# Norm gain on x, each token's norm at the exit of the projections, and x delivered transposed, in a hybrid retention and GLA layer

## The chip, the cores and the metric

The kernel runs on one core of a Trainium2 chip. The metric is the device time of one execution in microseconds (us), the median of three runs; a profile was taken of one further execution. Engines are named as in the profile: PE is the matmul engine (PEld its weight loads), DVE the vector engine, ACT the scalar engine, POOL the GpSimd engine, SP the engine that issues most DMAs.

## The reference

One layer over 512 tokens and 16 learned meta tokens ahead of them (528 rows of 1024 numbers), in float32:

```
u = x * rsqrt(mean(x*x) + eps) * norm_gain            # per token
rq, rk, rv, rg, gq, gk, gv, gg, glr, m_ret, m_gla = split(u @ w_in)
o_ret = groupnorm(retention(rope(rq), rope(rk), rv)) * silu(rg)          # 4 heads, 256 wide, values 512
log_a = log_sigmoid(glr @ w_gate_up + b_gate) / 16
o_gla = rmsnorm(gla(gq, gk, gv, log_a)) * silu(gg)                       # 4 heads, 128 wide, values 256
merged = sigmoid(m_ret) * (o_ret @ w_branch_ret) + sigmoid(m_gla) * (o_gla @ w_branch_gla)
out = rms_norm(x + merged @ w_out, final_norm_gain)[after the meta tokens]
```

The norm of a token is one number per row of u. It therefore commutes with every projection: (x * gain) @ w, scaled per row afterwards, is the same as u @ w.

## The kernel before

**Precision.** Every float32 product is done as three passes. `split` (L139 to L141) writes a rounded copy "hi" with ACT and the remainder "lo" with DVE; `mm3` (L151) or the loops in `quad` and `proj_a` then issue hi·hi, hi·lo and lo·hi. Tiles with `_h` and `_l` are such parts. `fh` and `fl` hold seven forms of the transposed activation (features on the 128 partitions, tokens along the row): three of its four blocks (`A11`, `A12`, `A22`; the fourth is `a21h`, `a21l`) and four sums of blocks (`S1` to `S4`).

**Projections.** `quad` (L198) does a 512-column projection with seven block products in place of eight, and needs the sums of blocks. `proj_a` (L276) and `proj_b` (L317) do plain projections and need the four blocks only. Products are pinned to a fixed order on PE; generators are woven by `weave`, so that small attention steps stand between large products. A scheduler fixes the order of the instructions of each engine when the program is built; on the chip each engine works through its list in that order.

**Start.** SP loads the five blocks of x and meta tokens, the gain (broadcast to all partitions, `ngb`) and the first weights `gv_w`. Per block (L432 to L455): ACT squares and sums a row (`sq`, `ss`), DVE and POOL turn the sum into 1/sqrt (`n_v`, `n_r`, L163 and L164), DVE multiplies the row by it and by the gain (`xn`, L439), PE transposes eight 128x128 pieces into PSUM (`xt`, L444), ACT and DVE split them into the forms and ACT keeps a plain copy `u` (L453). Then DVE makes the sums of blocks in tiles of their own (`s`, L472 to L475) and these are split. Beside this runs `gv0`, the first projection (`proj_b`, 96 matmuls of 512 columns), whose lo parts POOL makes (`gv_l`). It is followed by the gate's low-rank input `glr`, by `gq` and `gk` (`proj_a`, 96 matmuls each), with `forget_gates` (L483) woven in: `z` on PE, then Abs, Exp and Ln on ACT and the rest on DVE give `la`, the log of the forget gates.

**GLA and retention.** `gla_attention` (L604) needs `la`: matmuls `ge`, `gf` sum it, ACT takes exponentials (`gX`), DVE and POOL multiply by k and q (`gK`, `gQ`), PE makes scores `gc`. It is woven with `gg0`, a `quad` on columns of `gg`. Retention works per head: q, k with `rope`, the gate `rg`, scores (`ret_scores`, times a decay table), values `rv`, then `ret_attention`. `gates` (L931) makes `mr` and `mg` with four quads and multiplies the results onto the kept branch outputs (`kr`, `kg`, through DRAM). The output projection `wo` ends the kernel.

Of the kernel before, what the change touches and what calls it, by code (L numbers as in the profile page):

```python
# [18 lines left out]
F32 = mybir.dt.float32  # L20
# [86 lines left out]
def hybrid_kernel(ctx: ExitStack, tc: tile.TileContext, I, out: bass.AP):  # L107
# [18 lines left out]
    fh = [cp.tile([P, 4, HW], F32R, tag=f"fh{i}", name=f"fh{i}") for i in range(7)]  # L126
    fl = [cp.tile([P, 4, HW], F32R, tag=f"fl{i}", name=f"fl{i}") for i in range(7)]
# [3 lines left out]
    ggain = cp.tile([P, 16], F32, name="ggain")  # L131
# [7 lines left out]
    def split(hi, lo, src, eng=nc.vector):  # L139
        nc.scalar.copy(hi, src)  # L140
        eng.tensor_sub(lo, src, hi.bitcast(F32))  # L141
# [56 lines left out]
    def quad(cols, rows, name, evac, meta=None):  # L198
# [52 lines left out]
        nc.vector.tensor_sub(blk[0, 0], blk[0, 1], blk[0, 0])  # L251
# [23 lines left out]

    def proj_a(col, meta, name, evac):  # L276
# [33 lines left out]
    loaded = {}  # L310

# [5 lines left out]
    def proj_b(src, col, left, name, evac, meta=None):  # L317

        pss = [ppt(f"{name}_p{t}") for t in range(NTB)]
        psm = pat(f"{name}_pm") if meta is not None else None  # L320
        raws = []
        for q in range(4):
# [4 lines left out]
            if name == "gv0":  # L327
                for kk in range(2):
                    split(hi[:, kk, :], lo[:, kk, :], raw[:, kk, :], nc.gpsimd)
            else:  # L330
                split(hi, lo, raw)
            raws.append(raw)
# [9 lines left out]
            if psm is not None and q % 2 == 1:  # L342
                for g in range(4):
                    k = 2 * (q - 1) + g
                    nc.tensor.matmul(psm[32 * g:32 * g + 32], um[:, k, :], raws[q - 1 + g // 2][:, g % 2, :],
                                     start=q == 1, stop=q == 3)
            if q == 3 and psm is not None:
                late.append(lambda: meta(psm))
# [54 lines left out]
    gmask = g1.tile([P, 3, P], I32, name="gmask")  # L403

    xctx = ExitStack()
    xp = xctx.enter_context(tc.tile_pool(name="xp", bufs=2))


    blocks = [(I["x"][t * P:(t + 1) * P, :], P, t * P) for t in range(NTB)]
    blocks.append((I["meta_tokens"], NM, T))  # L410
    xts = []
    ngb = xp.tile([P, D], F32, name="ngb", bufs=1)
    for n, (src, rows, t0) in enumerate(blocks):
        xts.append(xp.tile([P, D], F32, tag="xt", name=f"xt{n}", bufs=5))
        nc.sync.dma_start(xts[n][:rows], src)
        if n == 0:
            nc.sync.dma_start(ngb, I["norm_gain"].to_broadcast([P, D]))
        if n < NTB:
            load_b(w_in, C_GV, n, "gv0")

    wzero = xp.tile([P, 512], mybir.dt.bfloat16, name="warm", bufs=1)
    nc.vector.memset(wzero, 0.0)
    wps = pat("warm_p")

    def warm(n):
        for _ in range(n):
            nc.tensor.matmul(wps, wzero[:, :P], wzero, start=True, stop=True)

    warm(14)
    nc.gpsimd.memset(um, 0.0)  # L430
    u = xp.tile([P, 2, 2, 4, HT], F32, name="u", bufs=1)
    for n, (src, rows, t0) in enumerate(blocks):  # L432
        xt = xts[n]
        sq = xp.tile([P, D], F32, tag="sq", name=f"sq{n}")
        ss = sp.tile([P, 1], F32, tag="ss", name=f"ss{n}")
        nc.scalar.activation(sq[:rows], xt[:rows], AF.Square, accum_out=ss[:rows])
        r = rstd_of(ss[:rows], D, rows, f"n{n}")
        xn = xp.tile([P, D], F32, tag="xn", name=f"xn{n}")
        nc.vector.scalar_tensor_tensor(xn[:rows], xt[:rows], r[:rows], ngb[:rows], op0=ALU.mult, op1=ALU.mult)  # L439
        for g in range(2):  # L440
            pt = pat(f"xt{n}_{g}")
            for e in range(4):
                k = 4 * g + e
                nc.tensor.transpose(pt[:, e * P:e * P + rows], xn[:rows, k * P:(k + 1) * P], ident[:rows, :rows])  # L444
            v = pt.rearrange("p (e t) -> p e t", e=4)[:, :, :rows]
            if rows == NM:
                nc.vector.tensor_copy(um[:, 4 * g:4 * g + 4, :NM], v)
                parts = [(th, 256, HT, v[:, :, HM * th:HM * (th + 1)]) for th in range(2)]
            else:
                parts = [(n // 2, (n % 2) * P, (n % 2 + 1) * P, v)]  # L450
            for th, c0, c1, w in parts:
                split(ah[th, g][:, :, c0:c1], al[th, g][:, :, c0:c1], w)
                nc.scalar.copy(u[:, th, g, :, c0:c1], w)  # L453
# [18 lines left out]
    nc.vector.tensor_sub(ss3, u[:, 0, 0], u[:, 1, 0])  # L472
# [604 lines left out]
```

## Time and profile before

| what | value |
|---|---|
| median of three runs | 822.9 us (822.75 to 823.49) |
| the profiled execution | 823.74 us, of which the span of the trace is 822.0 us |
| PE | busy 790.3 us (96%), 5466 matmuls |
| DVE | busy 541.5 us (66%) |
| ACT | busy 407.7 us (50%) |
| POOL | busy 147.3 us (18%) |
| granted PE clock, mean | 0.988 |
| DMA | 95.62 MB, 116 GB/s over the span |

The profile is one execution. Its page gives busy times, the span in 40 slices with the busy share of each engine in tenths, DMA queues, a chain of work followed back from the end, and the costliest groups of instructions. Further views used below: a table of stretches (busy time per engine in each), groups of instructions by line, and the instructions in order of time; there a row is start, duration, engine, line, operation, output<-input, and in brackets how long the engine was idle before and what ended it. In the chain's view a row is start, length and what, and since matmuls overlap in a pipeline, its lengths give the rate better than a single matmul's duration.

### The profile page before, as it was taken

Reading aid. Unit: us, or ns where it says so; the run is one execution under the profiler, and the core shown is the slowest. Engines: PE = TensorE matmul, PEld = TensorE weight load, DVE = VectorE, ACT = ScalarE, POOL = GpSimd, SP = SyncE. Lnnn points to the kernel's source line nnn. Section 1 sums busy time; section 2 is a strip of 40 time slices with the busy share of each in tenths; the row PEclk is TensorE's granted clock in tenths of the full one; section 3 lists DMA queues with packets and bytes.
Section 4 is the critical chain, followed back from the end, with each engine's and each line's share of the span. In section 5 each row is a group of like instructions: output and inputs, shape, how many; then the busy total and the mean of one; then the engine's idle time right before and its main releaser. Section 6 shows DMA issues by size and latency. Waiting matters only on the chain.

```text
span 822.0 us, 13635 instructions
## 1 busy us (share of the span) xinstructions
PE 790.3 (96%) x5466; PEld 719.3 (88%) x5466; DVE 541.5 (66%) x775; ACT 407.7 (50%) x673; POOL 147.3 (18%) x186
## 2 busy tenths in 40 slices
PE   6898999999999999999999999999999998999896
PEld 3687988998887999998999989999899998998685
DVE  3758666577643398766677576766757778885922
ACT  6564585357744336525445354453444555553422
POOL 4500243005331240013000141002410010021031
PEclk9998999999999999999999999999999999999999
DMA  9240330033335803521426237261472267589402
GB/s 282 82 115 26 90 90 3 26 103 103 111 120 143 193 26 103 176 82 65 143 76 185 72 72 151 66 198 57 85 146 71 84 218 230 179 184 249 146 0 103
DMA packets 84679, 95.62 MB, mean 116 GB/s; under 512 B 7988, under 2 KB 71732, under 8 KB 84616
## 3 DMA queue, kind: packets, MB, share of 16 engines
q1 hardware_dynamic: 78984, 86.36, 34.4%
q0 software_dynamic: 5632, 8.39, 7.0%
q8 instruction: 43, 0.70, 0.4%
q14 instruction: 20, 0.16, 0.1%
HBM read 77.96 MB, written 16.78 MB: 115 GB/s over the span
## 4 chain that ended last, share of the span: by engine, by line
PE 75%; DVE 6%; DMA 4%; ACT 4%; issue 2%; POOL 2%; SPq 0%; POOLq 0%; DVEq 0%; ACTq 0%
PE rk_p L297 6%; PE rg_b L225 6%; PE rq_p L297 6%; PE rv_b L225 5%; PE gk_p L297 3%; PE rg_c L225 3%; PE br_p L155 3%; PE br_p L152 3%; PE br_p L156 3%; PE rv_c L225 2%; PE mg_b L225 2%; DMA mk<-kept 2%; PE gg_b L225 2%; PE wo_p L152 2%; PE wo_p L156 2%
## 5 line engine op out<-in xcount | busy, mean ns | idle before, releaser
L164 POOL TENSOR_TENSOR g_r<-g_v,mhalf 128x1 f32<-128x1 f32 x16 | 10.3, 646 | 265.4 <-DVE g_v L163 265.4
L152 PE MATMUL br_p<-oh,br_h 128*128 128x512 f32 x128 | 50.1, 391 | 0.5 <-DVE mt L974 0.5
L155 PE MATMUL br_p<-ol,br_h 128*128 128x512 f32 x128 | 50.3, 393 | 0.0
L156 PE MATMUL br_p<-oh,br_l 128*128 128x512 f32 x128 | 50.1, 391 | 0.0
L141 DVE TENSOR_TENSOR rg_l<-rg_w,rg_h 128x1024 fp32r<-128x1024 f32 x24 | 30.0, 1252 | 17.9 <-ACT rg_h L140 17.9
L141 DVE TENSOR_TENSOR rv_l<-rv_w,rv_h 128x1024 fp32r<-128x1024 f32 x24 | 29.4, 1224 | 15.8 <-ACT rv_h L140 15.8
L914 ACT ACTIVATE on<-av,nm,g_r 128x512 f32<-128x512 f32 x16 | 12.5, 778 | 52.6 <-DVE nm L912 52.6
L140 ACT CAST rv_h<-rv_w 128x1024 fp32r<-128x1024 f32 x24 | 25.3, 1052 | 23.9 <-issue 7.3
L225 PE MATMUL rv_b<-rv_h,fh 128*128 128x256 f32 x128 | 36.3, 284 | 0.0
L225 PE MATMUL rg_b<-rg_l,fh 128*128 128x256 f32 x128 | 36.0, 281 | 0.0
L225 PE MATMUL rv_b<-rv_h,fl 128*128 128x256 f32 x128 | 36.0, 281 | 0.0
L225 PE MATMUL rv_b<-rv_l,fh 128*128 128x256 f32 x128 | 36.0, 281 | 0.0
L140 ACT CAST rg_h<-rg_w 128x1024 fp32r<-128x1024 f32 x24 | 25.2, 1052 | 21.6 <-PE br_p L155 11.6
L225 PE MATMUL rg_b<-rg_h,fl 128*128 128x256 f32 x128 | 35.9, 281 | 0.0
L225 PE MATMUL rg_b<-rg_h,fh 128*128 128x256 f32 x128 | 35.8, 280 | 0.0
L639 POOL COPY gto<-gX 128x1 f32<-128x1 f32 x16 | 8.5, 530 | 122.9 <-ACT gX L629 122.9
L152 PEld LDWEIGHTS br_p<-oh,br_h 128*128 128x128 f32 x128 | 24.0, 188 | 6.1 <-issue 0.9
L638 POOL TENSOR_TENSOR gQ<-gX,gq 128x512 f32<-128x512 f32 x16 | 28.3, 1768 | 3.9 <-ACT gX L631 3.9
L152 PE MATMUL wo_p<-wo_h,mh 128*128 128x512 f32 (+1 forms) x72 | 26.9, 374 | 2.0 <-DVE mt L974 2.0
L156 PEld LDWEIGHTS br_p<-oh,br_l 128*128 128x128 f32 x128 | 24.0, 188 | 5.2
L155 PEld LDWEIGHTS br_p<-ol,br_h 128*128 128x128 f32 x128 | 24.0, 188 | 5.0
L297 PE MATMUL rk_p<-fh,rk_h 128*128 128x264 f32 x96 | 27.6, 287 | 0.0
(490 smaller groups left out, 3098.2 us busy)
## 6 DMA issues: line engine op xcount, KB each, us to landing
rg_w<-in_w_in_dram SPq DMA_DIRECT2D x16, 512.0 KB, 4.2
rv_w<-in_w_in_dram SPq DMA_DIRECT2D x16, 512.0 KB, 3.9
br_w<-in_w_branch_ret_dram SPq DMA_DIRECT2D x16, 512.0 KB, 4.1
gv_w<-in_w_in_dram SPq DMA_DIRECT2D x8, 512.0 KB, 3.6
gg_w<-in_w_in_dram SPq DMA_DIRECT2D x8, 512.0 KB, 4.5
bg_w<-in_w_branch_gla_dram SPq DMA_DIRECT2D x8, 512.0 KB, 3.5
rq_w<-in_w_in_dram SPq DMA_DIRECT2D x8, 512.0 KB, 4.2
rk_w<-in_w_in_dram SPq DMA_DIRECT2D x8, 512.0 KB, 4.6
```

The lines of the kernel that those rows point to most:

```text
L140: nc.scalar.copy(hi, src)
L141: eng.tensor_sub(lo, src, hi.bitcast(F32))
L152: m = nc.tensor.matmul(o, lh, rh, start=first, stop=False)
L155: nc.tensor.matmul(o, lh, rl, start=False, stop=False)
L156: m = nc.tensor.matmul(o, ll, rh, start=False, stop=last)
L164: nc.gpsimd.tensor_tensor(r[:rows], v[:rows], mhalf[:rows], op=ALU.pow)
L225: m = nc.tensor.matmul(ps[:, t, :], l, r, start=first and j == 0, stop=kk == 3 and j == 2, skip_group_check=not fresh or t == 1)
L297: m = nc.tensor.matmul(pss[t][th], l[:, kk, c], r, start=first and j == 0, stop=kh == 1 and kk == 3 and j == 2, skip_group_check=not meta ...
L638: nc.gpsimd.tensor_mul(Q[b, h], X[:, 0:4, :], qb)
L639: nc.gpsimd.tensor_copy(TO[b, h], X[:, 0, P - 1:P])
L914: nc.scalar.activation(on, ps, AF.Identity, scale=r, bias=nm)
```

## The change

The host hands over x and the meta tokens a second time, transposed (`xt`, features on partitions), and the gains as columns. The projections read x times the norm's gain: ACT makes hi as gain times `xt`, DVE makes lo (gain times `xt` less hi) in one instruction. No token's norm is in them.

The norms are worked out beside this, from the untransposed x (`xr`): five Squares on ACT, one pair of instructions for all of them, and result `rt` (a column per block of tokens). Through DRAM (`rd`, then a broadcast, both DMAs issued by POOL) it also becomes `rb`, the norms along the row on all partitions. They are applied where a group leaves: in the scale of the ACT copy or Silu (`rows_into`, now two instructions of 128x256 in place of one of 128x512), in the copy of gq and gk and of `glr` (times `rb`), in the cosine and sine tables for rope, in the multiply by the decay table for the values of retention, and in a DVE multiply ahead of each Sigmoid of `gates`.

The transposes, their PSUM copies, `xn`, `ngb` and three warm-up matmuls go. `gv0` is written out at the start, its first three quarters with the products of one block of features first, lo parts by DVE. The block sums are made in `u` itself. Their splits are ordered behind the weight splits of `gq0`, and `sums` takes turns with `forget_gates`. In `forget_gates` one DVE addition goes to ACT and two DVE instructions become one. The small loads of the gate come early. `mh` and `ml`, at the end, lie in other tiles.

```diff
+    u = [xp.tile([P, 4, 2, HT], F32, name=f"u{i}") for i in range(2)]
+    nc.sync.dma_start(ng, I["norm_gain"])
+    for q in range(4):
+        raw = wraw(f"gv0_{q}_w", (P, 2, 512))
+        for s in (slice(0, 1), slice(1, 2)) if q == 0 else (slice(0, 2),):
+            k0, n = 2 * q + s.start, s.stop - s.start
+            nc.sync.dma_start(u[k0 // 4][:, k0 % 4:k0 % 4 + n], I["xt"][:, k0:k0 + n])
+            nc.sync.dma_start(raw[:, s], w_in[k0 * P:(k0 + n) * P, C_GV:C_GV + 512]
                              .rearrange("(k p) c -> p k c", p=P))
...
+    for n in range(NTB):
+        nc.sync.dma_start(xr[n], I["x"][n * P:(n + 1) * P, :])
+        if n % 2:
+            load_a(C_GQ, n // 2, "gq0")
...
-        nc.scalar.activation(sq[:rows], xt[:rows], AF.Square, accum_out=ss[:rows])
-        r = rstd_of(ss[:rows], D, rows, f"n{n}")
-        nc.vector.scalar_tensor_tensor(xn[:rows], xt[:rows], r[:rows], ngb[:rows], op0=ALU.mult, op1=ALU.mult)
-                nc.tensor.transpose(pt[:, e * P:e * P + rows], xn[:rows, k * P:(k + 1) * P], ident[:rows, :rows])
-                split(ah[th, g][:, :, c0:c1], al[th, g][:, :, c0:c1], w)
-                nc.scalar.copy(u[:, th, g, :, c0:c1], w)
+            nc.scalar.activation(xh[kh][:, k, :, :HT], u[kh][:, k], AF.Copy, scale=g)
+            nc.vector.scalar_tensor_tensor(xl[kh][:, k, :, :HT], u[kh][:, k], g, xh[kh][:, k, :, :HT].bitcast(F32),
+                                           op0=ALU.mult, op1=ALU.subtract)
+            split(hi[:, kk, :], lo[:, kk, :], raw[:, kk, :])
+        steps = [(t, kk) for t in range(NTB) for kk in range(2)]
+        if q < 3:
+            steps.sort(key=lambda x: x[1])
...
-    nc.vector.tensor_sub(ss3, u[:, 0, 0], u[:, 1, 0])
-    for i, s in ((S3, ss3), (S2, ss2), (S1, ss1), (S4, ss4)):
-        split(fh[i][:, :, :HT], fl[i][:, :, :HT], s)
+    nc.vector.tensor_add(u11, u10, u11)
+    nc.vector.tensor_sub(u10, u00, u10)
+    s2 = nc.vector.tensor_sub(u00, u11, u00)
+    nc.vector.tensor_sub(u01, u01, u00)
+    for n in range(NTB + 1):
+        nc.scalar.activation(xr[n], xr[n], AF.Square, accum_out=ss[:, n:n + 1])
+    nc.vector.tensor_scalar(ss, ss, 1.0 / D, EPS, op0=ALU.mult, op1=ALU.add)
+    nc.gpsimd.tensor_tensor(rt, ss, mhalf.to_broadcast([P, NTB + 1]), op=ALU.pow)
+    nc.gpsimd.dma_start(rd[0, :T].rearrange("(n p) -> p n", p=P), rt[:, :NTB])
+    nc.gpsimd.dma_start(rd[:, T:].rearrange("o m -> m o"), rt[:NM, NTB:])
+        nc.gpsimd.dma_start(rb[:, :, c * 256:c * 256 + w],
+                            rd[:, o:o + 2 * w].to_broadcast([P, 2 * w]).rearrange("p (h t) -> p h t", h=2))
...
+            nc.vector.tensor_mul(pr, ps[:, :HT], rb[:, s, :])
...
-            nc.scalar.activation(d, p if q is None else d, func)
+            for i in range(2):
+                nc.scalar.activation(d[:, i], p[:, i] if q is None else d[:, i], func,
+                                     scale=rt[:, 2 * th + i:2 * th + i + 1])
...
-    weave(run(gla_v(0), gla_qk(0)), forget_gates(), 4)
+    weave(gla_qk(0), turns(forget_gates(), sums()), 2)
...
-        nc.scalar.activation(dst, p if q is None else dst, AF.Sigmoid)
+        nc.vector.tensor_mul(dst, p if q is None else dst, rb[:, th, :256].unsqueeze(1).to_broadcast([P, 2, 256]))
+        nc.scalar.activation(dst, dst, AF.Sigmoid)
```

Three places show what the scheduler made of it. On ACT, ahead of the cast of the first weights of gq (`gq_0_h`), which PE needs after gv0; `s` are the block sums, `fh` their hi parts, `gv_p` the PSUM results of gv0. Before:

```order
L140 CAST gv_3_h<-gv_3_w 128x512
L453 COPY u<-xt_0_264 128x4x8
L453 COPY u<-xt_1_276 128x4x8
L140 CAST fh_85<-s_302 128x4x264
L140 CAST fh_83<-s_300 128x4x264
L140 CAST gq_0_h<-gq_w_575 128x1024
```

And now:

```order
L486 COPY gv_111<-gv_p_189 128x512
L486 COPY gv_111<-gv_p_190 128x512
L514 ACTIVATE xr_129,ss<-xr_129 128x1024
L514 ACTIVATE xr_123,ss<-xr_123 128x1024
L514 ACTIVATE xr_124,ss<-xr_124 128x1024
L152 CAST gq_0_h<-gq_w_163 128x1024
L152 CAST gvm_h<-gv_pm 128x512
L514 ACTIVATE xr_125,ss<-xr_125 128x1024
L514 ACTIVATE xr_126,ss<-xr_126 128x1024
```

The cast of gq's weights moved from ahead of the copies of gv0 to behind the last of them and behind three of the five Squares.

On ACT, ahead of the first exponentials of GLA's attention (`gX`); `fg_e` are the forget gates' tiles, `lah` the hi part of `la`, `gg_x` a copy of a partial result of gg0. Before:

```order
L140 CAST gk_1_h<-gk_w_771 128x1024
L536 ACTIVATE fg_e_555<-fg_e_555,one 128x512
L536 ACTIVATE fg_e_564<-fg_e_564,one 128x512
L595 COPY gq_571<-gq_p_573 128x512
L140 CAST gg_1_h<-gg_w_830 128x1024
L595 COPY gq_571<-gq_p_574 128x512
L536 ACTIVATE fg_e_616<-fg_e_616,one 128x512
L140 CAST lah_872<-la 128x256
L140 CAST lah_941<-la 16x256
L140 CAST gg_2_h<-gg_w_832 128x1024
L140 CAST gg_6_h<-gg_t_908 128x1024
L234 COPY gg_x_869<-gg_b 128x512
```

And now:

```order
L152 CAST gg_6_h<-gg_t_826 128x1024
L574 ACTIVATE fg_e_725<-z_723 128x512
L575 ACTIVATE fg_e_725<-fg_e_725 128x512
L585 ACT_TABLE_LOAD
L585 ACTIVATE fg_e_607<-fg_e_607,one 128x512
L577 ACTIVATE fg_z<-fg_e_725,one 128x512
L585 ACTIVATE fg_e_615<-fg_e_615,one 128x512
L585 ACTIVATE fg_e_681<-fg_e_681,one 128x512
L585 ACTIVATE fg_e_725<-fg_e_725,one 128x512
L585 ACTIVATE fg_e_689<-fg_e_689,one 128x512
L251 COPY gg_x_787<-gg_b 128x512
L152 CAST lah_790<-la 128x256
```

The logarithms and the first `lah` moved behind the cast of the third operand of gg0 (`gg_6_h`); before they stood among the casts of gk. In both programs the table load for `gX` follows (directly before; now after two more casts of gg0 and the meta part of `lah`).

On POOL, the new way of the norms between the cast of `sel` and the clearing of `stb`, where the program before had only the casts of `sel`, `gsum` and `gsm`:

```order
L531 CAST sel<-sel_raw 128x128
L516 TENSOR_TENSOR rt<-ss,mhalf 128x5
L517 DMA rd<-rt 128x4x1
L518 DMA rd<-rt 16x1
L532 CAST gsum<-gs_raw 128x640
L533 CAST gsm<-gsm_raw 16x16
L520 DMA rb<-rd 128x2x256
L520 DMA rb<-rd 128x2x8
```

Two DMAs to DRAM and two back, each pair behind the other, stand ahead of the first use of `rb` on DVE.

More of the change, by code (lines that the diff above doesn't have):

```diff
@@ L250, in quad @@
         product(2, A12, blk[1, 0], a, True)
-        nc.vector.tensor_sub(blk[0, 0], blk[0, 1], blk[0, 0])
+        t1 = nc.vector.tensor_sub(blk[0, 0], blk[0, 1], blk[0, 0])
+        if name == "gg0":
+            after(t1, marks["gl"])
         nc.vector.tensor_sub(t2, blk[1, 1], blk[0, 0])
@@ L326, in proj_b @@
             hi, lo = wsplit([P, 2, 512], f"{name}_{q}")
[L327 to L332, printed above, removed]
+            split(hi, lo, raw)
             for t in range(NTB):
@@ L341, in proj_b @@
                     yield
[L342 to L348, printed above, removed]
             yield
@@ L403, in hybrid_kernel @@
     gmask = g1.tile([P, 3, P], I32, name="gmask")
-    xctx = ExitStack()
[L406 to L419, printed above, removed]
@@ L421, in hybrid_kernel @@
-    wzero = xp.tile([P, 512], mybir.dt.bfloat16, name="warm", bufs=1)
+    gvm = [g1.tile([NM, 512], F32, tag="gvm", name=f"gvm{p}") for p in range(2)]
+    gv = [g1.tile([P, NTB, 512], F32, tag="gv", name=f"gv{p}") for p in range(2)]
+    gv0 = gv[0]
+    dp = ctx.enter_context(tc.tile_pool(name="dp", bufs=1, space=bass.MemoryType.DRAM))
+    kept = dp.tile([P, KD, T], F32, name="kept")
+    kept2 = dp.tile([P, KD, T], F32, name="kept2")
+    rd = dp.tile([1, TT], F32, name="rd")
+    gf = g1.tile([P, NTB, 512], F32, tag="goh", name="fg_f")
@@ L422, in hybrid_kernel @@
+    for n in range(NTB):
+        nc.sync.dma_start(xr[n], I["x"][n * P:(n + 1) * P, :])
+        if n % 2:
+            load_a(C_GQ, n // 2, "gq0")
+    wzero = xp.tile([P, 512], mybir.dt.bfloat16, name="warm")
     nc.vector.memset(wzero, 0.0)
     wps = pat("warm_p")
[L425 to L429, printed above, removed]
+    for _ in range(14):
+        nc.tensor.matmul(wps, wzero[:, :P], wzero, start=True, stop=True)
@@ new lines, in hybrid_kernel @@
+    for kh in range(2):
+        for k in range(4):
+            nc.scalar.activation(u[kh][:, k], u[kh][:, k], AF.Copy, scale=ng[:, 4 * kh + k:4 * kh + k + 1])
+        nc.vector.tensor_copy(um[:, 4 * kh:4 * kh + 4, :NM].rearrange("p k (h m) -> p k h m", h=2),
+                              u[kh][:, :, :, 256:HT])
+    psm = pat("gv0_pm")
+    for k in range(KD):
+        g = k % 4
+        nc.tensor.matmul(psm[32 * g:32 * g + 32], um[:, k, :], graw[k // 2][:, k % 2, :], start=k < 4, stop=k >= 4)
@@ L773, in hybrid_kernel, with turns @@
         nc.gpsimd.memset(stb[i], 0.0)
-    weave(run(gla_v(0), gla_qk(0)), forget_gates(), 4)
+    def turns(*gens):
+        gens = list(gens)
+        while gens:
+            for g in list(gens):
+                try:
+                    next(g)
+                    yield
+                except StopIteration:
+                    gens.remove(g)
+    weave(gla_qk(0), turns(forget_gates(), sums()), 2)
     weave(gla_g(0), gla_attention(0))
@@ L786, in hybrid_kernel @@
     nc.sync.dma_start(cs, I["rope"].rearrange("p c (h t) -> p c h t", h=2))
+    for i in range(2):
+        nc.vector.tensor_mul(cs[:, i], cs[:, i], rb)
     km = rp.tile([P, 2, P], F32R, name="km")
```

218 lines of the change are left out of this document (116 added, 102 removed).

## The prediction

> **What bounds the kernel now.** First the page: what each engine does over the span, and PE in 40 slices.
>
> ```profile
> span 822.0 us, 13635 instructions
> PE 790.3 (96%) x5466; PEld 719.3 (88%) x5466; DVE 541.5 (66%) x775; ACT 407.7 (50%) x673; POOL 147.3 (18%) x186
> PE   6898999999999999999999999999999998999896
> ```
>
> PE is the bound; it falls short at the start (a digit is 20.5 us), near digit 34 and at the end. So the question is how early PE gets through its first products. The table of stretches (columns: PE, weight loads, DVE, ACT, POOL busy, granted clock, DMA share, GB/s) shows the start:
>
> ```profile
> 10.00:30.00 20.00, 13.58 (x58) 10.15 (x59) 12.09 (x20) 14.51 (x31) 11.12 (x12) 0.84 0.64 183
> 30.00:52.00 22.00, 21.22 (x109) 16.72 (x109) 13.27 (x14) 9.96 (x22) 6.14 (x9) 0.99 0.30 81
> ```
>
> From 10 to 30 us PE has 58 matmuls, from 30 to 52 us 109. The rows in order of time (the first three) name what it waits for, and the chain (the rest) gives the pace and the end of gk:
>
> ```profile
> 10.89 0.50 PE L152 MATMUL gv_p<-gv_h,fh 128*128 128x512 f32 x1 [1.91 <-ACT fh L140]
> 69.75 0.39 PE L624 MATMUL ge<-gsum,lah 128*128 128x256 f32 x1 [2.36 <-ACT lah L140]
> 71.92 0.59 PE L297 MATMUL gk_p<-fh,gk_l 128*128 128x264 f32 x1 [1.33 <-DVE gk_l L141]
> 52.09 0.23 PE gv_p L152
> 52.78 0.99 PE gv_pm L345 x8
> 47.48 4.14 PE glr L511 x32
> 55.26 0.24 PE z L521
> 274.96 11.34 PE rq_p L297 x96
> 286.30 11.65 PE rk_p L297 x96
> 71.92 14.26 PE gk_p L297 x92
> 86.18 2.85 PE gg_b L225 x24
> ```
>
> The first product starts at 10.9 us, gk ends at 86.2 us. At full pace the 96 products of gv0 at 0.23 are 22.2 us; gv_pm twice 1.0; glr 4.1; gq and gk, of the shape of rq and rk, 11.3 and 11.7; five z at 0.24, 1.2; two matmuls of gvm_s, as wide as gv0's, 0.5. Together 53.0 us of PE work in a stretch of 75.3 us. The 22 us lost there are what the change can take.
>
> **The change part by part.** *First product.* The warm-up, and the first loads as ACT waits for them:
>
> ```profile
> 1.18 6.43 PE L427 MATMUL warm_p<-warm 128*128 128x512 bf16 x17 [1.18 <-DVE warm L422]
> 4.32 1.06 ACT L436 ACTIVATE sq<-xt 128x1024 f32<-128x1024 f32 x1 [2.32 <-DMA xt<-in_x_dram]
> 7.92 1.14 ACT L140 CAST gv_h<-gv_w 128x512 fp32r<-128x512 f32 x2 [2.46 <-DMA gv_w<-in_w_in_dram]
> ```
>
> A first 512 KB is usable at 4.3 us, a third at 7.9: 1.8 us each. The first block of features and its weights are 526 KB, so about 4.4; two casts on ACT and two lo parts on DVE, overlapping, at about 0.6 (half of the last row's pair) bring the first lo·hi to 6.5. The 14 warm-ups end at 6.9 (the 17 end at 7.6, three at 0.23 less). I take 6.9. Every later block comes after 1.8 us of loading and needs 1.2 of ACT's casts, 0.6 of ACT's scaling of u and 1.3 of DVE, while PE works 2.8 us on each: the loads and casts run ahead. So gv0 runs closed to 29.1, gv_pm to 31.2. The 40 transposes and their waits are gone.
>
> *Wait for gq's weights.* ACT has the last copy of gv0, from 29.2, then three Squares, then the cast:
>
> ```profile
> L579 ACT COPY gv<-gv_p 128x512 f32<-128x512 f32 x4 | 2.3, 582 | 3.8 <-PE gv_p L156 3.8
> L436 ACT ACTIVATE sq<-xt 128x1024 f32<-128x1024 f32 (+1 forms) x5 | 5.4, 1075 | 2.5 <-DMA xt<-in_x_dram 2.5
> 54.35 1.05 ACT L140 CAST gq_h<-gq_w 128x1024 fp32r<-128x1024 f32 x1
> 55.44 1.23 DVE L141 TENSOR_TENSOR gq_l<-gq_w,gq_h 128x1024 fp32r<-128x1024 f32 x1
> ```
>
> 29.2 + 0.5 + 3 x 1.05 + 1.05 = 33.9, and DVE's lo part to 35.2: PE, ready at 31.2, does four products in between and stands 3.5 us. That stall is new. From 35.2 it does 20 products at half pace (4.4; next step), gvm_s (0.9) and 24 at full (2.8), to 43.4. DVE goes on with rows of this kind:
>
> ```profile
> L141 DVE TENSOR_TENSOR fl<-s,fh 128x1056 fp32r<-128x1056 f32 x4 | 5.0, 1244 | 0.0
> 31.20 1.50 DVE L472 TENSOR_TENSOR s<-u 128x1056 f32<-128x1056 f32 x1 [0.42 <-ACT u L453]
> ```
>
> A sum 1.4, gvm_l 0.65, a sum 1.4, the norms' line 0.1 (38.7), one lo part 1.2 and gq's second lo 1.15: 41.0, in time for 43.4.
>
> *Clock after a stall.* Behind the two waits before 71.9 us, 92 products take 14.26 us, which at rk's pace are 11.16: 3.1 lost to a half clock. After the 3.5 us I take 2.4 (the 20 products and gvm_s above), between no loss and 3.1. [...]
>
> So gk ends at 6.9 + 53.0 + 3.5 + 2.4 = 65.8 us, 20.4 earlier.
>
> *Attention's start.* Here much is given back:
>
> ```profile
> L526 ACT ACTIVATE fg_e<-z 128x512 f32<-128x512 f32 x5 | 2.8, 597 | 0.1
> L528 ACT ACTIVATE fg_e<-fg_e 128x512 f32<-128x512 f32 x5 | 2.9, 638 | 0.0
> L536 ACT ACTIVATE fg_e<-fg_e,one 128x512 f32<-128x512 f32 x5 | 3.4, 719 | 0.0
> 89.66 1.28 ACT L629 ACT_TABLE_LOAD   x1
> 94.31 2.28 POOL L638 TENSOR_TENSOR gQ<-gX,gq 128x512 f32<-128x512 f32 x1
> 96.64 0.49 PE L648 MATMUL gc<-gQ,gK 128*128 128x128 f32 x2
> ```
>
> Before, the logarithms lay beside gk; now the fifth z stands behind gk, and all five behind that. ACT's instructions overlap by about 0.1, so from 65.8: gg_6_h 1.0, Abs and Exp 1.05, table load 1.3, five Ln and one addition 3.65, gg_x 0.5, lah 0.3, two casts of gg0 2.0, lah_860 0.25, in all 10.05: 75.8. The rest as before: from the load (89.66) to the scores of the second head (96.64) 7.0, so 82.8, behind 13.8 us of lead, with the same products of gg0 done. On the way PE has stood 1.7 us for lah and twice over 2 us for gQ; for half clock afterwards I take off 2 (0 to 3.1).
>
> *rb.* Nothing if it comes in time. POOL's transfers, a load of 4-byte pieces, and a power beside a full DVE:
>
> ```profile
> kept<-mt POOLq DMA_DIRECT2D x16, 256.0 KB, 5.4
> kept<-kg POOLq DMA_DIRECT2D x8, 256.0 KB, 6.2
> rgain<-in_ret_norm_gain_dram SPq DMA_DIRECT2D x1, 8.0 KB, 5.3
> 663.01 2.06 POOL L164 TENSOR_TENSOR g_r<-g_v,mhalf 128x1 f32<-128x1 f32 x1 [5.01 <-DVE g_v L163]
> ```
>
> The norms' line ends at 38.7; the power (0.6, at worst 2.1) and two trips of 5.4 give rb at 50.1. DVE gets there at 47.6 (from 41.0 three lo parts, gk_0_l, fg_r, gk_1_l) and waits, with the copies of gq and the lo parts of gg0 queued behind. From rb to the gate's operand is 2.7 us (two DVE and two ACT instructions of half width, twice, overlapping). PE comes to z at 56.0: from 43.4 24 products (2.8), glr (4.1), 24 (2.8), 24 of gk (2.9). The cover ends with rb at 53.3; two trips of 6.2 behind the slow power give 53.2. I take 0, at most 3.
>
> *gates.* Sixteen more DVE multiplies of 128x512, 0.6 apart, by the first two rows below (674.48 to 675.08). Then DVE's room there, and PE's one wait:
>
> ```profile
> 674.48 0.69 DVE L551 TENSOR_TENSOR sigr<-mr_b,mr_x 128x512 f32<-128x512 f32 x1
> 675.08 1.22 DVE L141 TENSOR_TENSOR mr_l<-mr_w,mr_h 128x1024 fp32r<-128x1024 f32 x1
> 675.00:690.00 15.00, 11.77 (x94) 11.15 (x93) 15.00 (x23) 10.07 (x17) 0.00 (x0) 0.97 0.79 243
> 690.00:740.00 50.00, 50.00 (x415) 50.00 (x415) 39.43 (x41) 26.65 (x34) 6.07 (x5) 0.97 0.71 186
> 689.35 0.58 PE L225 MATMUL mr_b<-fh,mr_l 128*128 128x256 f32 x1 [2.37 <-DVE mr_l L141]
> ```
>
> From 675 to 690 DVE is full and PE waits for it. Three multiplies come ahead of that `mr_l` (1.8), one difference of weights (1.1) now comes behind it; with a clock echo I take 1.5, from 0.5 to 9.8 (all sixteen, at most 0.61 each). After 690 DVE has 10.6 us free for 6.7.
>
> *The rest.* The halved copies and Silus (each pair at most one more ACT instruction, 0.6) lie on an engine half idle; a few stand in attention's chain, 0.5 (0 to 1). The multiply of the tables by rb and the decay with rt lie on DVE far ahead of PE's need or replace an instruction of the same size: 0.
>
> **Sum.** 13.8 - 2 - 1.5 - 0.5 = 9.8 us. The profiled execution took 823.7 us, 0.8 more than the median of 822.9; against the median 813.1: I predict 813.
>
> **Rivals.** *More of the 22 us is won* (19%): every wait above was taken in full. If the clock holds (2.4 and 2) and the wait for gq's weights is half as long (1.7), 807; if it vanishes, 805. Against it: the cast stands behind the Squares on ACT in fixed order.
>
> *rb comes late* (8%): POOL's transfers are held until DVE pauses. DVE has no pause from 36 to 47.6; from there two trips of 5.4 end at 58.4, the operand is there at 61.1, PE stands 5 us and loses up to 3 of clock: 818 to 821. For it, the slow power above; against it, the 5.4 and 6.2 us were met beside a DVE that is 79% busy in `gates`. [...]
>
> *Slower* (4%): the same place, if the two trips together take over 23 us, that is rb after 63: then the wait, 10 us behind the cover, eats the whole lead. At 15 us a trip rb comes at 69.3, 16 late, and with 3 of clock the time is 832. The 4-byte load's 5.3 us speaks against it.
>
> *DVE becomes the bound of gates* (9%): 79% busy there, and near full with four more multiplies in the 19.9 us of a quad (7 x 2.85). If half of the 9.8 us show, 816 to 817; all, 821.
>
> **How the numbers follow.** The forecast, with its own range of 809 to 816, has 60%. The range reaches to the rivals on both sides until 2 in 10 are left out: 805.5 to 819. A change under 0.2% (1.6 us) can't be told from none here. Faster 92%; same 4% (the last two cases at their ends); slower 4%.
>
> **What would show it.** The first product near 6.9 us and 96 of gv0 without a wait; 3 to 4 us of wait for ACT's and DVE's parts of gq; the end of gk near 66; waits of PE ahead of `ge` and twice ahead of `gc`; none ahead of `z`; a longer one in `mr_b`. The forecast is wrong if the first loads are usable only after 6 us, if PE waits at z, or if it waits in `mg`.

## The result and the profile after

The changed kernel takes 829.7 us (median of six runs, 826.0 to 832.0) where the kernel before takes 823.1 (821.9 to 823.5): a ratio of 1.0075 with a 95% interval of 1.0049 to 1.0102. It is slower by 6.6 us; 813 had been forecast, which is 10 us faster.

The profiled execution took 830.7 us. Its page, in the rows that answer to those of before:

```profile
span 828.7 us, 13576 instructions
PE 790.2 (95%) x5423; PEld 720.3 (87%) x5423; DVE 548.8 (66%) x784; ACT 420.7 (51%) x701; POOL 136.1 (16%) x179
PE   8878899999999999999999999999999998999796
PEclk9998899999999999999999999999999999999898
```

PE has the same busy time as before, with less work: 43 matmuls fewer. The slices show where: the first digit is fuller (8 for 6), but the third falls from 9 to 7, and of the last three the first falls from 8 to 7. The clock is short of full speed near the end and at two digits of the start. The table of stretches and the rows in order of time (start, duration, engine, line, operation, and in brackets the idle time and what ended it) for the start:

```profile
10.00:30.00 20.00, 20.00 (x87) 15.88 (x85) 10.97 (x17) 15.53 (x27) 0.00 (x0) 1.00 0.85 288
30.00:52.00 22.00, 18.60 (x141) 16.75 (x141) 13.70 (x13) 15.64 (x24) 5.69 (x6) 0.92 0.53 158
6.83 0.49 PE L169 MATMUL gv_p<-gv_h,xh 128*128 128x512 f32 x1 [0.59 <-ACT gv_h L152]
34.85 0.39 PE L323 MATMUL gq_p<-xh,gq_h 128*128 128x256 f32 x1 [2.88 <-ACT gq_h L152]
60.97 1.20 PE L569 MATMUL z<-fg_r 128*128 128x512 f32 x2 [5.08 <-DVE fg_r L564]
63.39 0.59 PE L323 MATMUL gk_p<-xh,gk_h 128*128 128x264 f32 x1 [1.23 <-DVE gq L626]
60.00:66.00 6.00, 3.80 (x14) 3.12 (x15) 4.98 (x9) 5.05 (x11) 0.00 (x0) 0.50 0.00 1
250.00:255.00 5.00, 4.93 (x15) 3.70 (x15) 1.13 (x3) 1.06 (x2) 0.29 (x1) 0.66 0.21 73
82.19 0.39 PE L242 MATMUL gg_b<-gg_h,fh 128*128 128x256 f32 x1 [2.06 <-ACT gg_x L251]
91.95 0.49 PE L680 MATMUL gc<-gQ,gK 128*128 128x128 f32 x2 [2.20 <-POOL gQ L670]
```

The first product stands at 6.83 us, 87 matmuls run in the stretch that held 58, and there is one wait of 2.88 for gq's weights: so far it goes as forecast. Then PE waits 5.08 us at `z`, the first product that hangs on `rb` (the norms along the row), and 1.23 behind it, and from 60 to 66 us its clock is 0.50.

Following the same products in both traces gives the lead of the changed kernel along the program (start or end of the named products in the rows in order of time; us):

| point | before | after | lead | forecast |
|---|---|---|---|---|
| end of gv0 | 52.78 | 30.12 | 22.7 | 23.7 |
| end of gk | 86.18 | 74.22 | 12.0 | 20.4 |
| scores of the second head | 96.64 | 91.95 | 4.7 | 13.8 |
| start of the branch product bg | 218.97 | 214.88 | 4.1 | 11.8 |
| start of rq | 274.80 | 273.42 | 1.4 | 11.3 |
| start of mr | 650.08 | 648.86 | 1.2 | 11.3 |
| end of mg | 744.73 | 746.54 | -1.8 | 9.8 |
| last product of wo | 815.34 | 822.19 | -6.9 | 9.8 |

Three places lose: the wait at `z` (8.4 us), the gates and the tail behind them (8.1 us), and 2.7 us in bg, where the clock from 250 to 255 us is 0.66. A kernel that differs from before only behind 650 us (d_before_mul, below) took 1.5 us longer than before for the same products, so this last loss varies from kernel to kernel and from execution to execution, and is put down to no part of the change; of all traces the kernel before's own is the quickest there.

In the tail, first rows of PE, of DVE and of the table of stretches; then, in part, the chain of work that ended last (start, length, what):

```profile
732.29 0.39 PE L242 MATMUL mg_b<-fh,mg_l 128*128 128x256 f32 x1 [1.29 <-DVE mg_l L153]
777.18 0.79 PE L169 MATMUL wo_p<-wo_h,mh 128*128 128x512 f32 x1 [2.97 <-DVE mt L1023]
722.86 0.69 DVE L988 TENSOR_TENSOR kg<-kg,mg 128x512 f32<-128x512 f32 x1 [2.05 <-DMA kg<-kept]
749.00 0.69 DVE L988 TENSOR_TENSOR kg<-kg,mg 128x512 f32<-128x512 f32 x1 [3.85 <-DMA kg<-kept]
761.10 0.69 DVE L1024 TENSOR_TENSOR mt<-mt,mk 128x512 f32<-128x512 f32 x1 [3.02 <-DMA mk<-kept]
778.00:788.00 10.00, 10.00 (x34) 7.88 (x34) 6.50 (x8) 2.42 (x4) 0.00 (x0) 0.74 0.00 0
```

```profile
742.30 1.23 DVE br_l L153
743.55 0.37 SPq L338
743.96 0.47 SPq L987
...
744.83 4.74 DMA kg<-kept
749.61 1.23 DVE br_l L153
750.86 5.39 DMA wo_w<-in_w_out_dram
756.26 0.62 DVE mt L1023
756.88 6.50 DMA wo_w<-in_w_out_dram
```

This is a ring. DVE's `br_l` frees a weight buffer, SP may then issue a load of wo's weights (L338), behind it in SP's queue stands the load of a kept row (L987), DVE stands behind that load with the next `br_l` in its line, and that frees the next buffer. Every trip in it, 4.7 to 6.5 us long, is on the path.

### The profile page after: what moved, and what is told of

Read it like the earlier page. It is cut to its first block, busy times and chain, and to the rows that moved or that the text cites. A ratio compares the mean times of both kernels' runs of the same rounds, so it can differ in the third digit from the quotient of the medians.

```text
span 828.7 us, 13576 instructions
## 1 busy us (share of the span) xinstructions
PE 790.2 (95%) x5423; PEld 720.3 (87%) x5423; DVE 548.8 (66%) x784; ACT 420.7 (51%) x701; POOL 136.1 (16%) x179
## 4 chain that ended last, share of the span: by engine, by line
PE 69%; DVE 12%; DMA 5%; issue 5%; ACT 5%; POOL 2%; SPq 0%; POOLq 0%; DVEq 0%; ACTq 0%
PE rk_p L323 6%; PE rq_p L323 5%; PE rg_b L242 5%; PE rv_b L242 5%; PE rg_c L242 3%; PE br_p L172 3%; PE br_p L169 3%; PE br_p L173 3%; PE rv_c L242 2%; DMA kg<-kept 2%; PE wo_p L169 2%; PE wo_p L172 2%; PE wo_p L173 2%; PE bg_p L172 2%; PE bg_p L173 2%
## 5 line engine op out<-in xcount | busy, mean ns | idle before, releaser
L323 PE MATMUL rk_p<-xh,rk_h 128*128 128x264 f32 x128 | 37.2, 290 | 0.0
L323 PE MATMUL rk_p<-xl,rk_h 128*128 128x264 f32 x128 | 36.4, 284 | 0.0
L323 PE MATMUL rk_p<-xh,rk_l 128*128 128x264 f32 x128 | 36.2, 283 | 0.0
L323 PE MATMUL rq_p<-xh,rq_l 128*128 128x256 f32 x128 | 36.1, 282 | 0.0
L323 PE MATMUL rq_p<-xl,rq_h 128*128 128x256 f32 x128 | 36.0, 282 | 0.0
L323 PE MATMUL rq_p<-xh,rq_h 128*128 128x256 f32 x128 | 35.8, 280 | 0.0
L172 PE MATMUL wo_p<-wo_l,mh 128*128 128x512 f32 (+1 forms) x72 | 27.7, 385 | 0.0
L173 PE MATMUL wo_p<-wo_h,ml 128*128 128x512 f32 (+1 forms) x72 | 27.6, 383 | 0.0
```

Source lines behind the costliest of these rows:

```text
L172: nc.tensor.matmul(o, lh, rl, start=False, stop=False)
L173: m = nc.tensor.matmul(o, ll, rh, start=False, stop=last)
L323: m = nc.tensor.matmul(pss[t][th], l[:, kk, c], r, start=first and j == 0, stop=kh == 1 and kk == 3 and j == 2, skip_group_check=not meta ...
```

## The experiments: rb

**a_rb_one.** The norms along the row are a constant, there from the start.

```diff
+    nc.gpsimd.memset(rb, 1.0)
...
-    nc.gpsimd.dma_start(rd[0, :T].rearrange("(n p) -> p n", p=P), rt[:, :NTB])
-    nc.gpsimd.dma_start(rd[:, T:].rearrange("o m -> m o"), rt[:NM, NTB:])
...
-        nc.gpsimd.dma_start(rb[:, :, c * 256:c * 256 + w],
...
```

> The changed kernel with rb set to ones by POOL at the start: the two trips through DRAM and the wait for them are gone (the norm's factor along the tokens is left out of the result). Theory 'late rb': the wait of 5.1 us ahead of z, the 1.2 us behind it and some 3 us of slow clock are what ate the lead, so the time falls by 8 to 9, from 829.7 to about 821. Rival 'the chain of ACT and DVE ahead of the first scores is long anyway': the logarithms, the casts of gg0 and the tables take the same time, PE just waits at ge and gQ instead of at z, and the time falls by 3 at most, to 827 or more.

Measured: 819.5 us, 0.9958 of before [0.9944, 0.9973], 10.3 under the changed kernel. The two rows of PE at `z` (nothing waited for) and at the second head's scores:

```profile
56.13 0.62 PE L565 MATMUL z<-fg_r 128*128 128x512 f32 x2
83.67 0.49 PE L676 MATMUL gc<-gQ,gK 128*128 128x128 f32 x2 [2.20 <-POOL gQ L666]
```

gk ends at 65.95, 8.3 us sooner, and this lead over the changed kernel is the same at every product up to mr. So at the start the late rb is what ate the lead. Four more kernels below keep this way of making rb (c, g, k and l, by their first letters). In their traces PE waits 2.4 to 3.9 us at `z`, and gk ends at 71.5 to 73.7: there the late rb costs 5.5 to 7.7 us, and the changed kernel's profiled execution, with 8.3, is the dearest of the five.

**b_rb_sp.** The four transfers of rb by SP.

```diff
+    for kh in range(2):
+        load_a(C_GK, kh, "gk0")
...
-    nc.gpsimd.dma_start(rd[0, :T].rearrange("(n p) -> p n", p=P), rt[:, :NTB])
+    nc.sync.dma_start(rd[0, :T].rearrange("(n p) -> p n", p=P), rt[:, :NTB])
...
```

> The changed kernel with the four small transfers that make rb issued by SP instead of POOL (gk's two weight loads are put ahead of them, so that they don't wait). Theory 'held on POOL': the first trip, 12.1 us from issue to landing on POOL, takes 4 to 5 us on SP, rb is there near 51 instead of 58.5, and the time falls by 5 to 8, to 822 to 825. Rival 'pieces of 4 bytes are slow by themselves': the trip takes about 12 us on SP too, rb comes after 57, and the time stays within 2 of 829.7.

Measured: 828.0 us, 1.0055 [1.0040, 1.0069]. The first trip took about 9 us on SP (8.9 for its small second piece, the only one whose landing the trace gives; the readers were issued 9.1 after the first piece), neither 4 to 5 nor 12, and the edit had a cost of its own: the small loads behind it in SP's queue waited, and PE stood 6.1 us for `sel`. Inconclusive on the cause, so the trip was measured alone.

**m_trip.** Four trips alone, in a program of their own.

> A small program of four trips of the kind rd and rb make (128x4 pieces of 4 bytes to DRAM, 2 KB from there to all partitions): by POOL with DVE idle, by POOL with DVE busy for 28 instructions of 128x1056, by SP with DVE idle, by SP with DVE busy. It computes nothing of the reference. Theory 'held by DVE': by POOL the first leg takes 4 to 6 us with DVE idle and lands only after DVE's last instruction (over 25 us) with DVE busy; by SP 4 to 6 both times. Rival 'pieces of 4 bytes are slow': 9 to 12 us in all four.

Measured, in the view of DMA issues (queue, count, size, us to landing), in the order of the expectation:

```profile
rd<-rt POOLq DMA_DIRECT2D x1, 2.0 KB, 11.9
rd<-rt POOLq DMA_DIRECT2D x1, 2.0 KB, 8.3
rd<-rt SPq DMA_DIRECT2D x1, 2.0 KB, 8.4
rd<-rt SPq DMA_DIRECT2D x1, 2.0 KB, 10.7
```

With DVE full, POOL's transfer landed after 8.3 us, in the middle of DVE's 28 instructions. "Held by DVE" falls; the trip is slow from either queue, idle or not (the 11.9 ran beside four stores of 512 KB).

**m_piece.** The same 2 KB in pieces of other sizes.

> A small program of four trips by SP with all engines idle: 2 KB to DRAM as 512 pieces of 4 bytes, as 128 pieces of 16 bytes, as one piece of 2 KB, and once more as one piece, read back in 512 pieces of 4 bytes instead of to all partitions. It computes nothing of the reference. Theory 'pieces of 4 bytes': the first write takes 8 to 12 us, the second and third 3 to 5, the last read 4 to 6. Rival 'a write to DRAM takes that long as such': 8 to 12 for all three writes.

Measured: the 512 pieces of 4 bytes (beside the end of four stores, which the 8.3 and 8.4 above were not), the 128 pieces of 16 bytes, and the read of 4-byte pieces:

```profile
rd<-rt SPq DMA_DIRECT2D x1, 2.0 KB, 10.5
rd<-rt SPq DMA_DIRECT2D x1, 2.0 KB, 1.4
r<-rd SPq DMA_DIRECT2D x1, 2.0 KB, 2.1
```

The write as one piece of 2 KB was followed by its reader 1.1 us after its issue. So it is not the write to DRAM and not 4-byte pieces as such: it is writing 4-byte pieces. Reading the same pieces costs a fifth to a quarter. (The 16-byte write has a quarter as many pieces too; how much is size and how much number was not parted, but the read has all 512.)

**f_rb_pe.** rb without DRAM: ones times a diagonal of the norms on PE.

```diff
+        nc.vector.tensor_mul(dg.rearrange("p (n q) -> p n q", n=NTB), ident.unsqueeze(1).to_broadcast([P, NTB, P]),
+                             rt[:, :NTB].unsqueeze(2).to_broadcast([P, NTB, P]))
...
+                nc.tensor.matmul(pb, ones, dg, start=True, stop=True)
+                nc.scalar.copy(rb[:, :, :256], pb.rearrange("p (h t) -> p h t", h=2))
...
```

> The changed kernel with rb made without DRAM: two products of a tile of ones with the norms laid on a diagonal, placed behind the two halves of glr, and two copies on ACT. If the late rb is all that is lost at the start, PE meets no wait over 1 us ahead of z, gk ends near 66.5 (74.2 before this edit, 66.0 with rb set to ones) and the time falls by 7 to 10, to 820 to 823. Rival: the diagonal, one DVE instruction, and the copies come too late behind the casts, PE stands 3 us at glr instead, and the time falls by 4 at most.

Measured: 821.4 us, 0.9984 [0.9972, 0.9997]: 8.3 back of 10.3. `z` waits for nothing; what it costs is a wait of 0.86 for the diagonal, the product (1.10) and that of the meta tokens (0.39), and gk ends at 68.3.

## The experiments: the gates

**c_no_gate_mul** takes the sixteen multiplies out of the changed kernel (the edit shown), and **d_before_mul** puts such multiplies, by a tile of ones, into the kernel before.

```diff
-        nc.vector.tensor_mul(dst, p if q is None else dst, rb[:, th, :256].unsqueeze(1).to_broadcast([P, 2, 256]))
-        nc.scalar.activation(dst, dst, AF.Sigmoid)
+        nc.scalar.activation(dst, p if q is None else dst, AF.Sigmoid)
```

> The changed kernel without the sixteen multiplies in the gates (Sigmoid reads the sum or the PSUM as before the change; the norm's factor is left out there). Theory 'DVE bounds the gates': the 3.5 us lost in mg and the 5 lost behind it, in br and wo, come back, 829.7 falls by 7 to 9, to about 821.5. Rival 'the tail is lost to something else' (the new places of mh and ml, the transfers of kept): only the 3.5 us of mg come back, 826 or more, and the waits ahead of wo stay at 3 us.

> The kernel before with sixteen multiplies by a tile of ones put into the gates where the change puts them; nothing else is changed. Theory 'DVE bounds the gates': 823.1 rises by 7 to 9, to about 831, with waits of PE in mg and ahead of wo. Rival 'the multiplies alone cost what the prediction said': 1.5 more, 824 to 825, and the rest of the loss at the end belongs to other parts of the change.

Measured: without them 818.3 us, 0.9942 [0.9924, 0.9960], 11.4 less; with them the kernel before takes 829.3, 1.0076 [1.0058, 1.0093], 6.2 more. Of the 11.4 the trace puts 8.5 behind the start of mr; the rest lies ahead of it, where the two kernels are alike, and is scatter (in c's execution rb's first trip took 9.1 us in place of 12.1). PE's longest wait in wo, in d and then in c:

```profile
777.88 0.50 PE L152 MATMUL wo_p<-wo_h,mh 128*128 128x512 f32 x1 [3.72 <-DVE mt L977]
767.17 0.50 PE L169 MATMUL wo_p<-wo_h,mh 128*128 128x512 f32 x1 [1.28 <-DVE mt L1022]
```

In d PE waits 1.3 us in mg and 3.7 there, much as in the changed kernel (1.3 and 3.0); in c it waits nowhere in mg and 1.3 there, as in the kernel before. So the multiplies do it; the new places of `mh` and `ml`, which c keeps, do not. Their size varies with the execution: from the start of mr to the last product of wo the kernels with all sixteen and late loads of the kept rows take 169.5 to 173.3 us (a, b, d, f and the changed kernel, which is the dearest), the kernel before 165.3 and c 164.8.

**k_mul_mr.**

```diff
...
-        nc.vector.tensor_mul(dst, p if q is None else dst, rb[:, th, :256].unsqueeze(1).to_broadcast([P, 2, 256]))
-        nc.scalar.activation(dst, dst, AF.Sigmoid)
+        if name == "mr":
+            nc.vector.tensor_mul(dst, p if q is None else dst, rb[:, th, :256].unsqueeze(1).to_broadcast([P, 2, 256]))
+            nc.scalar.activation(dst, dst, AF.Sigmoid)
+        else:
+            nc.scalar.activation(dst, p if q is None else dst, AF.Sigmoid)
...
```

> The changed kernel with the eight multiplies in mr and none in mg (the norm's factor is left out there). Theory 'the last eight do it': those in mg stand right ahead of the last products and push DVE's line into br and wo; with them gone the time is that of the kernel with none, 818 to 820. Rival 'each costs the same': half of 11.4 comes back, 824.

Measured: 821.0 us, 0.9983 [0.9968, 0.9998]. By the medians the eight in mg cost 8.7 and the eight in mr 2.7 (821.0 against 818.3); the traces, from the start of mr on, put 8.1 on those in mg and 0.4 on those in mr. What costs is not how many, but where: ahead of the tail.

**g_pool.**

```diff
-            nc.vector.tensor_mul(k, k, g)
+            nc.gpsimd.tensor_mul(k, k, g)
```

> The changed kernel with the gates' sixteen multiplies by the kept rows (kr, kg) on POOL, which stands idle there; the sixteen by rb stay on DVE. So DVE has as many instructions in the gates as before the change, and no longer stands behind the transfers of kept. Theory 'DVE's line bounds gates and tail': the 8.5 us lost from mr on come back, 820 to 822. Rival 'POOL is no free room': its multiplies beside a full DVE take over 2 us each, slow DVE down, and hold back the transfers behind them on its queue: 826 to 832.

Measured: 830.1 us, 1.0096 [1.0073, 1.0118]; the rival. Three instructions of DVE of one kind, and POOL's pair, which begins while the first of them runs and lies beside the other two:

```profile
702.86 1.21 DVE L271 TENSOR_TENSOR mg_t<-mg_w,mg_w 128x1024 f32<-128x1024 f32 x1
704.00 2.33 DVE L276 TENSOR_TENSOR mg_w<-mg_w,mg_w 128x1024 f32<-128x1024 f32 x1
706.25 2.29 DVE L280 TENSOR_TENSOR mg_w<-mg_w,mg_t 128x1024 f32<-128x1024 f32 x1
703.09 4.37 POOL L988 TENSOR_TENSOR kr<-kr,sigr 128x512 f32<-128x512 f32 x2 [4.17 <-ACT sigr L978]
```

The first, begun ahead of POOL's pair, takes the 1.2 us that all of them take in the changed kernel; the two begun beside it take nearly twice as long. PE waits 2.9 to 3.8 us for lo parts three times. The tail, in turn, is mended (wo 47.7 us long in place of 51.0): DVE no longer stands behind the kept rows there. **h_both** adds the edit of f to it:

> Both edits together, rb by products and the multiplies by kept rows on POOL. If the two losses are independent the gains add: 829.7 less 8 to 10 and less 8 to 9 is 811 to 813, near the 813 forecast for the change itself. If they share a cause (the clock, the same transfers), it stays at 817 or more.

Measured: 827.4, 1.0056 [1.0040, 1.0072], only 2.7 under g. The sum failed with g's own gain; and of the 4.6 us by which PE is ahead of g at the end of gk, 2.0 are left at rq, since this execution ran the scores and bg at a slower clock (0.84 to 0.88 from 70 to 90 us and 0.83 from 240 to 250, where g had 1.00).

**l_kg_early.** The kept rows are loaded ahead; `cv` is the tile of the rotary tables. DVE's work stays as it is.

```diff
-            nc.sync.dma_start(k, src)
...
+        def early(src, j, name, q):
+            for i, (n, th) in enumerate(((0, 0), (1, 1))):
+                load(src, j, name, n, th, cv[:, 512 * i:512 * i + 512].rearrange("p (a b) -> p a b", a=2))
+            for i, _ in enumerate(q):
+                if i == 3:
+                    for n, th in ((0, 1), (1, 0)):
+                        load(src, j, name, n, th, tmp2(f"{name}{j}{n}{th}"))
+                yield
...
```

> The changed kernel with the kept rows (kr, kg) loaded ahead: the first two of each quad at its start into the tile of the rotary tables, which is free by then, the other two at its fourth product. No instruction of DVE is added or taken away. Theory 'DVE stands behind transfers': in the changed kernel DVE waits 2.0 us for kg at 720.8 and 3.9 at 745.2 with work queued behind; without these waits 3 to 6 of the 8.5 us come back, 824 to 827. Rival 'DVE simply has too much to do': the waits go elsewhere and the time stays at 829 to 830.

Measured: 816.7 us, 0.9935 [0.9910, 0.9961], 13.0 under the changed kernel, twice the most expected. First the sums from 640 us to the end for the changed kernel, then for this one, then PE's only wait ahead of wo here:

```profile
sum 359.00, PE 171.74 PEld 155.35 DVE 131.28 ACT 83.37 POOL 21.31; mean PE 171.74 PEld 155.35 DVE 131.28 ACT 83.37 POOL 21.31
sum 359.00, PE 165.05 PEld 150.44 DVE 131.09 ACT 82.41 POOL 21.33; mean PE 165.05 PEld 150.44 DVE 131.09 ACT 82.41 POOL 21.33
768.55 0.50 PE L169 MATMUL wo_p<-wo_h,mh 128*128 128x512 f32 x1 [0.85 <-DVE mt L1040]
```

DVE does the same 131 us of work and PE is done sooner. With the same work, then, it is DVE's waits for the kept rows that cost; how much of the 13.0 belongs to the multiplies, the next two runs tell.

**p_before_early** and **r_before_mul_early** put the early loads into the kernel before, without and with the multiplies, to part the two.

> The kernel before, with the kept rows loaded ahead as in the run of the changed kernel with early loads; nothing else. If the early loads only mend what the multiplies broke, the kernel before has nothing to mend: 822.9 less 0 to 2. Rival: they are a gain by themselves, whatever the change: 822.9 less 6 or more, to 817 or below.

> The kernel before with the sixteen multiplies by ones (829.3 with these alone) and with the kept rows loaded ahead. Theory 'the multiplies cost only through the loads behind which DVE stands': no more than 1 above the kernel before with early loads alone. Rival 'DVE's work itself': 3 or more above it.

Measured: 817.2 us, 0.9940 [0.9927, 0.9953], and 820.8, 0.9980 [0.9972, 0.9989]. The early loads are a gain of 5.7 by themselves: the ring was there before the change and cost then too. By the medians the multiplies cost 3.6 with the loads ahead (820.8 less 817.2) and 6.2 without. The traces, from the start of mr to the last product of wo, part them more sharply:

| kernel before | late loads | early loads |
|---|---|---|
| without the multiplies | 165.26 | 161.44 |
| with the multiplies | 171.11 | 162.05 |

There the multiplies cost 5.9 us with the ring and 0.6 without it. For r, then, the medians speak for the rival (3 or more) and the traces for the theory (1 at most). So 2.6 (medians) to 5.2 (traces) of their 6 us come through the ring. Where the rest lies is open: the profiled executions with early loads took 819.6 and 820.6 us, so their traces hold only 1.0 of the 3.6. Nor do the runs part the links of the ring: the early loads come sooner, use another tile, and stand elsewhere in SP's queue, all at once.

## The experiments: both together

**j_neither** applies the edits of a and c together.

> The changed kernel with rb set to ones and without the sixteen multiplies in the gates (both factors of the norm are left out there): what the change would be without the two costs. If they are independent, 829.7 less 10.3 and less 11.4 is 808; the prediction's own sum without its 1.5 for the gates says 811.5. Rival: part of what each edit alone gave back was the same slow clock, then 813 to 816.

Measured: 813.6, 0.9901 [0.9877, 0.9926]. With both costs gone the changed kernel is 2 us above the prediction's own sum of 811.5; the gains of a and c (10.3 and 11.4) come to 16.1 together, not 21.7. The single traces of the changed kernel give the two places 8.3 and 8.5, and 16.8 fits. But the two costs do not simply add: put into j one at a time, by the medians, the late rb costs 4.7 (818.3 in c) and the multiplies 5.9 (819.5 in a), 10.6 together, and both at once cost 16.1. The 5.5 between is put down to neither; the traces show both places at their dearest in the changed kernel's profiled execution, and why is open.

**n_best** is f and l together:

> The edit that makes rb by products of ones with a diagonal, and the earlier loads of the kept rows, together. If the earlier loads give 3 to 6, 821.4 falls to 816 to 818, faster than both kernels; if they give nothing, it stays at 821.

Measured: 813.5, 0.9888 [0.9864, 0.9911], below the expected 816 to 818.

**q_best2** replaces the diagonal:

```diff
+        for t in range(NTB):
+            nc.tensor.matmul(pb[:, t * P:(t + 1) * P], rt[:, t:t + 1].to_broadcast([P, P]), ident, start=True, stop=True)
...
```

> The changed kernel with early loads of the kept rows, and rb made by four products of the norm's column, spread over 128 columns, with the identity (no diagonal on DVE). PE's wait of 0.85 us for the diagonal goes and the product of 1.96 us becomes about 1.0: 813.5 less 1 to 2, to 811.5 to 812.5. Rival: these products are cheap on paper only (each loads its own weights) and it stays at 813 to 814.

Measured: 811.2, 0.9867 [0.9846, 0.9888]: faster than both kernels, with the whole computation in it. The page's first rows, and PE's row of the four products (two matmul instructions each):

```profile
span 807.4 us, 13588 instructions
PE   9898899999999999999999999999999998999996
46.11 1.05 PE L542 MATMUL rb<-ident,rt 128*128 128x128 f32 x8
```

The expectation's 1.96 was a misreading: in f it is the wait of 0.86 and the product of 1.10 together. So the rival was right about the products, which cost about the same. gk ends 1.3 us sooner than in f, of which 0.9 is that wait. It ends 1.2 sooner than in n, where the wait was only 0.34; 0.7 of that lies ahead of these products, where n ran at a slower clock (0.50 from 35 to 40 us, 0.66 here).

Against the kernel before with early loads (817.2) the change, so mended, is worth 6.0 us by the medians.

## Why the prediction was wrong

**Right:** the first product (6.9 forecast, 6.83), gv0 without a wait, the wait for gq's weights (3.5, measured 2.88 and 0.53), and PE's arrival at z (56.0, measured 55.89). Of the three waits forecast ahead of the scores two came, 2.06 us for `gg_x` at a product of gg0 and 2.20 for `gQ` at `gc`; none came at `ge`, and the lead lost behind them was 0.6, not 2. With rb in time, gk ended at 65.95 (65.8 forecast) and the second head's scores stood at 83.67 (82.8). The term of 13.8 measured 13.0 there. The half clock taken after a stall shows in the traces as 0.50 from 72 to 76 us before and from 60 to 66 now; behind the wait for gq's weights it was 0.66 from 35 to 40 us.

**The step that failed first: "rb. I take 0, at most 3."** It measured 8.3 us in the profiled execution (5.5 to 7.7 in the other four with this path), and 10.3 by the median of a. Not the order on the engines was misread but one price. The power ended at 41.3, half a microsecond past the latest that was allowed. The trips were costed at 5.4 each, from rows of 256 KB moved in long pieces, and a load of 4-byte pieces (5.3) was called in as a witness. The changed kernel shows 12.1 for the first and 3.8 to 4.2 for the second:

```profile
39.23 2.06 POOL L516 TENSOR_TENSOR rt<-ss,mhalf 128x5 f32<-128x5 f32 x1 [7.31 <-DVE ss L515]
41.60 1.00 POOL L517 DMA_DIRECT2D rd<-rt  x1 [0.31 <-POOL rt L516]
53.97 1.45 POOL L520 DMA_DIRECT2D rb<-rd  x2 [9.04 <-DMA rd<-rt]
rd<-rt POOLq DMA_DIRECT2D x1, 2.0 KB, 12.1
```

No row of before had a write of 4-byte pieces, and a read was taken in its place. PE was where the cover had it, at z at 55.9; DVE took rb up at 59.28, and 1.7 us from there to z (2.7 had been allowed) make the wait of 5.08. In c, g, k and l the first trip took 8.5 to 9.3 us and the second 5.3 to 6.3: there too the two together cost 14.3 to 15.3 us, not 10.8. The step's own upper end of 3 did not hold.

**Its rival had the right size and the wrong cause.** "rb comes late" said 5 us of wait and up to 3 of clock; measured 5.1, 1.2 and 2.1. But nothing was held until DVE paused: in m_trip POOL's transfer landed after 8.3 us beside a full DVE. That transfers wait for a pause of DVE was an assumption of the rival; no run here shows one that was held.

**The second: "gates ... 1.5", and "After 690 DVE has 10.6 us free for 6.7".** It measured 8.5 in the trace of the profiled execution, and 4.6 to 6.2 in four others with the same multiplies (a, b and f against c, d against the kernel before). The rival "DVE becomes the bound of gates" had allowed for all of it (9%), as work and not as waits. Counted as busy time the sentence was right. But free time of an engine that works through a list is room only if it is not a wait for something the engine itself sets going. In the kernel before, from 690 to 770 us, the view of waits (engine and line, what it waited for, us in total, times, longest) has these rows for DVE and, from 700 to 775, for SP:

```profile
DVE kg L939 <- DMA kg<-kept: 7.3, 3, 4.9
SPq L314 <- DVE br_l L141: 10.1, 3, 5.4
```

DVE waits for `kg`, and SP, which issues the loads of `kg`, waits for DVE. The multiplies moved DVE's releases later, so the loads came later too: 6.2 us in the kernel before, 3.6 without the ring (by the traces 5.9 and 0.6).

**Not costed at all: the tail.** The prediction ended with mg. Of the 8.1 us lost from mr on, 5.0 lie in br and wo (lead -1.8 to -6.9), through `mk` and `mt`, and 778 to 788 us ran at a clock of 0.74.

In sum: 813.9 forecast for the profiled execution, 8.3 for rb, 7.0 more for gates and tail make 829.2; it took 830.7. That the sum comes so close is partly luck, since in this execution both places were dearer than in the other traces with the same instructions there. The wrong sign came from two terms that were both taken near zero. For the gates the true size lay inside the term's bounds, for rb only in a rival of 8%; the two together lay outside the range, which had no case with both.

## What to carry to other kernels

The price of 2 KB here hung on its pieces and its direction (8.3 to 12.1 us written in pieces of 4 bytes, 1.4 in pieces of 16, 2.1 read in pieces of 4): for a transfer find a row with both, or give the price a wide range, above all where a cover of 3 us is all there is. One number per token gets to all partitions in 1.05 us on PE, and a copy out of PSUM on ACT (0.57), with the identity as the moving operand and the column spread as weights. Before idle time of an engine is spent, look at what ended each idle piece; where it was a transfer whose issue waits for that engine, load ahead first, which here was worth 5.7 us in the kernel before, nearly as much as the mended change (6.0).

## What the runs showed of the hardware

Writing 2 KB to DRAM in pieces of 4 bytes took 8.3 to 12.1 us in ten measurements on two queues, in pieces of 16 bytes 1.4, and reading it in pieces of 4 bytes 2.1. Why the 4-byte writes take so long, no run shows.

In g_pool a DVE difference of two float32 tiles of 128x1024 took 1.21 us where it began ahead of POOL's multiplies, and 2.33 and 2.29 where it began while one ran.
